# Between two expert layers: every group of tokens coded, POOL scaling all second one-hots, first one-hots of 8 tokens at once on DVE, GELU on 32 tokens

## Chip, cores and metric

One Trainium2 chip, one of its cores. The metric is the device time of one execution in microseconds (us), the median of the runs shown. Engines: PE (TensorE), DVE (VectorE), ACT (ScalarE), POOL (GpSimd) and SP, whose queue here only issues transfers.

## What is computed

256 tokens of width 2048 in f32 go through one block: norm and input projection, pooling and RG-LRU mixers, output projection, and then a retrieval layer over 16,384 experts, the part that matters here:

```python
i1, i2 = top-16 of two score vectors of 128 each      # 8 heads; 128 (i1, i2) pairs per token
expert = i1 * 128 + i2
act    = gelu(einsum('chkd,cd->chk', peer_u[expert], zc))
w      = gate * act
out    = einsum('chk,chkd->cd', w, peer_v[expert])
```

## The kernel before, in words

The kernel doesn't gather most of `peer_u` and `peer_v`. The u layer multiplies z with all 16,384 experts (columns 0 to 1535 as dense matmuls, the rest by gathers) and leaves a table `sw` in SBUF: 128 partitions (first index i1) by 256 tokens by 128 (second index i2). The v layer multiplies such a table, holding the weights, with all of `peer_v`. Between the two, the stage that the diff touches, each token's 128 scores are picked out of its 128x128 square, GELU and gate give 128 weights, and a new square holding the weights at their (i1, i2) is written back to `sw`. Nothing of the v layer's matmuls starts before the last square is written.

The stage works on groups q of 4 tokens, NQ = 64 groups. A loop over steps g does, in an order written out by hand, for group g the picking and for group f = g - LAG the forming:

- `onehot_t(q)`: the first-index one-hot of a group (partition = i1, column = slot) from `ibt`, a copy of the indices broadcast to all partitions by `load_ib` (SP queue). POOL does it by `is_equal` (L874), ACT by Abs and Relu for the groups in `OHT_ACT` (L871, L872). It is issued six groups ahead into five buffers of 8 tokens.
- `extract_mm(q)`: for each token a f32 matmul (two PE instructions) of its one-hot with its square, L940, gives PSUM `exb` [slot, i2]. In two groups of three (`CODED`) a second, bf16 matmul L944 adds an eight-row code (`code_buf`, loaded by `load_code` on SP) times a table, which pushes every column but the wanted one far down.
- `extract_pick(q)`: for a coded group one DVE maximum over the columns for 4 tokens (L952); otherwise for each token a DVE comparison with i2, product and sum (L956).
- `gelu_1`, `gelu_1s`, `gelu_2`, `gelu_2s`, `gelu_3` (L965 to L987): small DVE and ACT instructions for each TB = 16 tokens.
- `one_1(q)`: slot-major one-hot of i1, [128, 4, 128], on ACT for three groups of four (four Abs L998, one Relu L999), else one DVE comparison (L1001). `two_a`, `two_b`: the one-hot of i2 times the weight: for half of the groups DVE compares (L1009) and POOL multiplies (L1016), else four DVE instructions do both (L1020). Both go into `ott`, three buffers each.
- `form_mm(f)`: four f32 matmuls of the two one-hots (L1026), and `form_out(f - 1)`: ACT copies the squares from PSUM to `sw` (L1030).

Each engine runs its instructions in the order issued. `O1_LAST`, `O2_LAST` choose the engines of the last LAG = 8 groups.

Of the kernel before, what the change touches and what calls it, by code (L numbers as in the profile page):

```python
# [16 lines left out]
OP = mybir.AluOpType  # L17
# [25 lines left out]
TB = 16  # L43
LAG = 8
O1_ACT, O2_POOL = (1, 1, 1, 0), (1, 0)
O1_LAST, O2_LAST = (1, 0), (1, 1, 1, 0)
DOT_END = 12
NCODE, FAR = 8, 2.0 ** 120
CODED = (0, 1, 1)
V_MORE, ROOM = 10, 32  # L50
OHT_ACT = (4, 5, 8, 9)
# [103 lines left out]
def kernel(ctx: ExitStack, tc: tile.TileContext, x, cols, front, gates_w, keys, u1, u2, v1, v2,  # L155
# [711 lines left out]
    def onehot_t(q):  # L867

        o, ib = oht(q), ibt[:, q % 4]
        if q in OHT_ACT:  # L870
            nc.scalar.activation(o, ib, AF.Abs, scale=-1.0, bias=pidx)  # L871
            nc.scalar.activation(o, o, AF.Relu, scale=-1.0, bias=1.0)  # L872
        elif q < NQ:
            nc.gpsimd.tensor_scalar(o, ib, pidx, None, op0=OP.is_equal)  # L874
# [3 lines left out]
    for pr in range(64):  # L878
        acc = [bank("mm", 4) for _ in range(2)]
        for kg in range(GU):  # L880
# [15 lines left out]
            if u == nu - DOT_END + 1:  # L896
                assert done[0] == 256
                ibt = zbpool.tile([128, 4, 4, 128], BF, name="ibt", tag="zbhi")
                ohts.append(zbpool.tile([128, 8, 128], F32, name="ohta", tag="zblo"))
                ohts.append(gp.tile([128, 8, 128], F32, name="ohtb", tag="gat"))  # L900
                for q in range(4):
                    load_ib(q)
                for q in range(4):
                    onehot_t(q)
# [10 lines left out]
    pick = asw[:, 3, :].rearrange("p (a b) -> p a b", a=2)  # L915
# [12 lines left out]
    code_buf = [t.rearrange("p a b c -> p (a b c)").bitcast(BF) for t in (i1f, i2f)]  # L928
    coded = [q for q in range(NQ) if CODED[q % len(CODED)]]

    def load_code(n):
        if n < len(coded):
            nc.sync.dma_start(code_buf[n % 2][:NCODE], code_dram[:, coded[n] * 4:coded[n] * 4 + 4, :].rearrange("k t s -> k (t s)"))

    def extract_mm(q):
        p = psE.tile([128, 4, 128], F32, name="exb", bufs=4)
        for j in range(4):
            t = q * 4 + j
            far = q in coded
            nc.tensor.matmul(p[:, j, :].rearrange("p (b i) -> p b i", i=SB), oht(q)[:, j, :], swb[:, :, t, :],  # L940
                             start=True, stop=not far)
            if far:
                n = coded.index(q)
                nc.tensor.matmul(p[:, j, :], code_buf[n % 2][:, j * 128:(j + 1) * 128], ctab, start=False, stop=True)  # L944
        if far:
            load_code(n + 2)
        exb[q] = p

    def extract_pick(q):
        p = exb.pop(q)  # L950
        if q in coded:
            nc.vector.tensor_reduce(act[:, q * 4:q * 4 + 4], p, AX.X, OP.max)  # L952
            return
        for j in range(4):
            t = q * 4 + j
            nc.vector.scalar_tensor_tensor(pick[:, t % 2, :], iota, i2t[:, t:t + 1], p[:, j, :], op0=OP.is_equal,  # L956
                                           op1=OP.mult, accum_out=act[:, t:t + 1])

    gel = {}
    ctab = tv.rearrange("p a b c -> p (a b c)").bitcast(BF)[:, 18 * TB:18 * TB + NK]  # L960
    nc.gpsimd.memset(ctab, 0.0)
    nc.scalar.activation(ctab[:NCODE], wtok[:NCODE, 0, :], AF.Copy)
    gtmp = tv.rearrange("p a b c -> p (a b c)")[:, :9 * TB].rearrange("p (k t) -> p k t", k=9)

    def gelu_1(b):  # L965
        s = slice(b * TB, (b + 1) * TB)
        gel[b] = a, g, c = [gtmp[:, (b % 3) * 3 + j, :] for j in range(3)]
# [3 lines left out]
    def gelu_1s(b):  # L971
        a, g, c = gel[b]
        nc.scalar.activation(g, a, AF.Square)

    def gelu_2(b):
        a, g, c = gel[b]
        nc.vector.tensor_scalar(g, g, GELU_C, 1.0, op0=OP.mult, op1=OP.add)
        nc.vector.tensor_tensor(g, g, a, op=OP.mult)
# [10 lines left out]
    def pick_by(q, most, last):  # L989
        return last[(q - NQ + LAG) % len(last)] if q >= NQ - LAG else most[q % len(most)]  # L990

    def one_1(q):

        o = ott[:, q % 3]
        if pick_by(q, O1_ACT, O1_LAST):
# [3 lines left out]
            nc.scalar.activation(o, o, AF.Relu, scale=-1.0, bias=1.0)  # L999
        else:  # L1000
            nc.vector.tensor_tensor(o, iota[:, None, :].to_broadcast([128, 4, 128]),  # L1001
                                    i1t[:, q * 4:q * 4 + 4].unsqueeze(2).to_broadcast([128, 4, 128]), op=OP.is_equal)

    def o2_pool(q):
        return q >= 6 and pick_by(q, O2_POOL, O2_LAST)

    def two_a(q):
        if o2_pool(q):
            nc.vector.tensor_tensor(ott[:, 3 + q % 3], iota[:, None, :].to_broadcast([128, 4, 128]),  # L1009
                                    i2t[:, q * 4:q * 4 + 4].unsqueeze(2).to_broadcast([128, 4, 128]), op=OP.is_equal)  # L1010

    def two_b(q):

        o = ott[:, 3 + q % 3]
        if o2_pool(q):
            nc.gpsimd.tensor_tensor(o, o, wt[:, q * 4:q * 4 + 4].unsqueeze(2).to_broadcast([128, 4, 128]), op=OP.mult)  # L1016
        else:
            for j in range(4):
                t = q * 4 + j
                nc.vector.tensor_scalar(o[:, j, :], iota, i2t[:, t:t + 1], wt[:, t:t + 1], op0=OP.is_equal,  # L1020
                                        op1=OP.mult)
# [15 lines left out]
    for t in (i1f, i2f):  # L1037
        nc.gpsimd.memset(t, 0.0)
    load_code(0)
    load_code(1)  # L1040
    G = TB // 4
    for g in range(NQ + LAG + 2):
        if g == 0:
            onehot_t(4)
            onehot_t(5)
# [16 lines left out]
        onehot_t(g + 6)  # L1062
        load_ib(g + 8)
        if 0 <= f + 2 < NQ:
            two_a(f + 2)
        if 0 <= f < NQ:
# [218 lines left out]
```

## Time and profile before

| what | value |
|---|---|
| median of 3 runs | 1655.18 us (1652.76 to 1657.89) |
| profiled execution, its time | 1648.98 us |
| its span | 1647.2 us |
| PE, DVE, ACT, POOL busy over the span | 96%, 84%, 54%, 57% |
| the stage between the layers | about 940.8 to 1106.4 us, 165.6 us |

The profiled execution lies 6.2 us below the median. Shares of the whole span say little of this stage, which has one window of its own in the profile: it begins with the first picking matmul (L940) at 940.8 us, the last picking matmul is at 1086.1 us, and the v layer's first ACT instruction (L1117) is at 1106.38 us.

### The profile page before, as it was taken

The page shows a single profiled execution, that of the slowest core. Times are in us where ns is not written, and L with a number is a line of the kernel's source. Part 1 is how long each engine was busy: PE and PEld are TensorE (multiplying, and loading weights), DVE is VectorE, ACT ScalarE, POOL GpSimd, SP SyncE. Part 2 cuts the span into 40 slices and gives each one's busy share as a digit, 9 for nine tenths or more (in the row PEclk, how much of TensorE's full clock was granted, in tenths as well). Part 3 has the DMA queues.
Part 4 walks back from the last instruction along what each step waited for, and adds up shares of the span by engine and source line. Part 5 has one row for each costly group of instructions (what it writes and reads, how often), then busy time and mean ns, then how long its engine had stood idle before and what let it go on. Part 6 is the DMA issues. An engine that isn't in the chain of part 4 may idle for free.

```text
span 1647.2 us, 29352 instructions
## 1 busy us (share of the span) xinstructions
PE 1585.9 (96%) x10646; PEld 1461.2 (89%) x10646; DVE 1378.8 (84%) x2647; ACT 886.1 (54%) x1283; POOL 937.7 (57%) x790
## 2 busy tenths in 40 slices
PE   8899999999999999999999999979999999999996
PEld 8899888989999999999999988878888888888885
DVE  7799755999999997777777499977899998989897
ACT  6665544444444445445444578864545555555554
POOL 2486201346557766555553288846767765666663
PEclk9999999999999999999999999989999999999998
DMA  7455666568988888999998622209999999999992
GB/s 255 150 168 179 204 206 190 180 210 273 313 284 284 276 289 308 325 310 310 306 312 284 199 67 59 57 19 315 313 334 341 350 334 357 360 337 329 351 320 104
DMA packets 129137, 418.43 MB, mean 254 GB/s; under 512 B 18392, under 2 KB 28976, under 8 KB 128864
## 3 DMA queue, kind: packets, MB, share of 16 engines
q1 hardware_dynamic: 86784, 278.52, 51.4%
q0 software_dynamic: 42208, 138.05, 23.7%
q8 instruction: 83, 1.36, 0.3%
q14 instruction: 62, 0.51, 0.1%
HBM read 411.71 MB, written 4.78 MB: 253 GB/s over the span
## 4 chain that ended last, share of the span: by engine, by line
PE 82%; DVE 13%; ACT 2%; issue 1%; POOL 1%; DMA 1%; SPq 0%; ACTq 0%; DVEq 0%; POOLq 0%
PE mm L355 15%; PE mm L354 15%; PE mm L353 15%; PE acc L1144 10%; PE acc L1146 10%; PE acc L1145 10%; DVE ott L1020 3%; DVE lo L109 3%; PE mm L579 2%; PE mm L577 2%; PE mm L578 2%; DVE asw L956 1%; DVE asw L952 1%; DVE ott L1009 1%; ACT hi L108 1%
## 5 line engine op out<-in xcount | busy, mean ns | idle before, releaser
L108 ACT ACTIVATE hi<-raw 128x1024 fp32r<-128x1024 f32 x389 | 411.9, 1059 | 498.4 <-PE mm L354 348.2
L109 DVE TENSOR_TENSOR lo<-raw,hi 128x1024 fp32r<-128x1024 f32 x389 | 504.5, 1297 | 180.2 <-ACT hi L108 178.4
L355 PE MATMUL mm<-zahi,lo 128*128 128x256 f32 x2016 | 574.2, 285 | 15.2 <-DVE lo L109 15.1
L353 PE MATMUL mm<-zahi,hi 128*128 128x256 f32 x2016 | 574.4, 285 | 0.0
L354 PE MATMUL mm<-zalo,hi 128*128 128x256 f32 x2016 | 572.5, 284 | 0.0
L1095 POOL DMA_INDIRECT gatv<-in_v_dram,e x256 | 333.6, 1303 | 178.9 <-DVE accg L1105 114.7
L355 PEld LDWEIGHTS mm<-zahi,lo 128*128 128x128 f32 x2016 | 388.8, 193 | 18.0 <-DVE lo L109 17.8
L353 PEld LDWEIGHTS mm<-zahi,hi 128*128 128x128 f32 x2016 | 389.2, 193 | 0.0
L354 PEld LDWEIGHTS mm<-zalo,hi 128*128 128x128 f32 x2016 | 389.1, 193 | 0.0
L1144 PE MATMUL acc<-hi,wht 128*128 128x512 f32 x512 | 200.3, 391 | 1.8 <-ACT wht L1117 1.8
L1146 PE MATMUL acc<-hi,wlt 128*128 128x512 f32 x512 | 200.3, 391 | 0.0
L1145 PE MATMUL acc<-lo,wht 128*128 128x512 f32 x512 | 200.3, 391 | 0.0
L1105 DVE SCALAR_TENSOR_TENSOR accg<-gatv,wtok,accg 128x512 f32<-128x512 f32 x252 | 183.3, 749 | 2.0 <-DMA gatv<-in_v_dram,e 2.0
L678 POOL DMA_INDIRECT sw<-in_u_dram,e x96 | 112.0, 1167 | 93.0 <-DVE sw L688 46.1
L1144 PEld LDWEIGHTS acc<-hi,wht 128*128 128x128 f32 x512 | 96.6, 189 | 22.2 <-ACT wht L1117 2.1
L1145 PEld LDWEIGHTS acc<-lo,wht 128*128 128x128 f32 x512 | 96.7, 189 | 20.7 <-DVE lo L109 0.6
L1146 PEld LDWEIGHTS acc<-hi,wlt 128*128 128x128 f32 x512 | 96.6, 189 | 20.5 <-DVE wlt L1118 0.6
L1144 PE MATMUL acc<-more,wht 128*128 128x512 f32 x256 | 99.8, 390 | 0.0
L1145 PE MATMUL acc<-more,wht 128*128 128x512 f32 x256 | 99.6, 389 | 0.0
L1146 PE MATMUL acc<-more,wlt 128*128 128x512 f32 x256 | 99.6, 389 | 0.0
L1026 PE MATMUL fob<-ott 128*128 128x128 f32 x512 | 79.1, 296 | 15.7 <-DVE ott L1020 5.4
L678 POOL DMA_INDIRECT gatzbhi<-in_u_dram,e x54 | 61.3, 1136 | 48.2 <-DVE gatzbhi L688 32.6
(288 smaller groups left out, 2729.0 us busy)
## 6 DMA issues: line engine op xcount, KB each, us to landing
raw<-in_u_dram SPq DMA_DIRECT2D x192, 512.0 KB
raw<-in_v_dram SPq DMA_DIRECT2D x125, 512.0 KB
raw<-in_front_dram SPq DMA_DIRECT2D x114, 512.0 KB
sw<-in_v_dram SPq DMA_DIRECT2D x67, 512.0 KB
ibt<-i_dram SPq DMA_DIRECT2D x64, 128.0 KB
gatv<-in_v_dram,e POOLq DMA_INDIRECT x256, 5.9
xh<-in_x_dram SPq DMA_DIRECT2D x8, 256.0 KB
h_dram<-xh POOLq DMA_DIRECT2D x8, 256.0 KB, 3.5
```

What stands on the lines that cost most here:

```text
L108: nc.scalar.activation(s[1], r[1], AF.Copy)
L109: nc.vector.tensor_tensor(s[2], r[1], s[1].bitcast(F32), op=OP.subtract)
L353: nc.tensor.matmul(o, ah, bh, start=first, stop=False)
L354: nc.tensor.matmul(o, ah, bl, start=False, stop=False)
L355: nc.tensor.matmul(o, al, bh, start=False, stop=last)
L678: nc.gpsimd.indirect_dma_start(out=g, out_offset=None, in_=u2, in_offset=bass.IndirectOffsetOnAxis(ap=e32[:, i, sl:sl + 1], axis=0))
L1026: nc.tensor.matmul(p[:, j, :], ott[:, q % 3, j, :], ott[:, 3 + q % 3, j, :], start=True, stop=True)
L1095: nc.gpsimd.indirect_dma_start(out=g, out_offset=None, in_=v2, in_offset=bass.IndirectOffsetOnAxis(ap=e32[:, i, s:s + 1], axis=0))
L1105: nc.vector.scalar_tensor_tensor(a, g, wtok[:, i, s:s + 1], a, op0=OP.mult, op1=OP.add)
L1144: nc.tensor.matmul(acc[i][c], whi[:, j, ts], vh[:, s], start=first, stop=False)
L1145: nc.tensor.matmul(acc[i][c], whi[:, j, ts], vl[:, s], start=False, stop=False)
L1146: nc.tensor.matmul(acc[i][c], wlo[:, j, ts], vh[:, s], start=False, stop=last)
```

## The change

All groups are coded, with four code buffers in place of two, and `extract_pick` is always the one DVE maximum. The second one-hot is for every group a DVE comparison (`two_a`) and a POOL product (`two_b`). The first-index one-hots are made for 8 tokens at once and, but for the first ones (POOL, in the u layer) and the pairs at groups 4 and 8 (ACT), on DVE. The slot-major one-hot of i1 has a third way, "s": POOL subtracts i1 from the column numbers (`one_0`, one step ahead), ACT does Abs and Relu on all 512 columns at once; "a" is the way on ACT alone, "d" the DVE comparison. The groups before the last 12 follow "ssassasd" by q modulo 8 (33 "s", 13 "a", 6 "d"), the last 12 follow "add" by q modulo 3 (4 "a", 8 "d"). GELU takes 32 tokens, in five DVE instructions for six, and LAG grows from 8 to 12.

```diff
--- before.py
+++ after.py
@@ -40,15 +40,14 @@
 GVBUFS = 6
 VIEW_I2 = 64
 SB = 32
-TB = 16
-LAG = 8
-O1_ACT, O2_POOL = (1, 1, 1, 0), (1, 0)
-O1_LAST, O2_LAST = (1, 0), (1, 1, 1, 0)
+TB = 32
+LAG = 12
+O1_BY, O1_LAST = "ssassasd", "add"
+NCB = 4
 DOT_END = 12
 NCODE, FAR = 8, 2.0 ** 120
-CODED = (0, 1, 1)
 V_MORE, ROOM = 10, 32
-OHT_ACT = (4, 5, 8, 9)
+OHT_ACT = (4, 8)
 UNIT_NS, LO_NS, DOT_NS = 2600, 1140, 670
 BUDGET = UNIT_NS - LO_NS
 NG1, GFIRST = 6, 96
@@ -864,14 +863,17 @@
     def oht(q):
         return ohts[q // 2 % NOHT][:, q % 2 * 4:q % 2 * 4 + 4]
 
-    def onehot_t(q):
-
-        o, ib = oht(q), ibt[:, q % 4]
+    def onehot_t(q, eng=None):
+
+        if q >= NQ:
+            return
+        o = ohts[q // 2 % NOHT].rearrange("p a b -> p (a b)")
+        ib = ibt[:, q % 4:q % 4 + 2].rearrange("p a b c -> p (a b c)")
         if q in OHT_ACT:
             nc.scalar.activation(o, ib, AF.Abs, scale=-1.0, bias=pidx)
             nc.scalar.activation(o, o, AF.Relu, scale=-1.0, bias=1.0)
-        elif q < NQ:
-            nc.gpsimd.tensor_scalar(o, ib, pidx, None, op0=OP.is_equal)
+        else:
+            (eng or nc.vector).tensor_scalar(o, ib, pidx, None, op0=OP.is_equal)
 
     nu = 64 * GU
     done0 = done[0]
@@ -900,8 +902,8 @@
                 ohts.append(gp.tile([128, 8, 128], F32, name="ohtb", tag="gat"))
                 for q in range(4):
                     load_ib(q)
-                for q in range(4):
-                    onehot_t(q)
+                for q in (0, 2):
+                    onehot_t(q, nc.gpsimd)
             if u == nu - 3:
                 for q in range(4, 8):
                     load_ib(q)
@@ -912,7 +914,6 @@
 
     asw = cst.tile([128, 4, T], F32, name="asw", tag="zg")
     act, sgt, wt = asw[:, 0, :], asw[:, 1, :], asw[:, 2, :]
-    pick = asw[:, 3, :].rearrange("p (a b) -> p a b", a=2)
     p = bank("tp", 2)
     for i in range(2):
         nc.tensor.transpose(p[:, i * 128:(i + 1) * 128], sg[:, i, :], ident)
@@ -925,57 +926,45 @@
     ott = zpool.tile([128, 6, 4, 128], F32, name="ott", tag="zalo")
 
     exb, fob = {}, {}
-    code_buf = [t.rearrange("p a b c -> p (a b c)").bitcast(BF) for t in (i1f, i2f)]
-    coded = [q for q in range(NQ) if CODED[q % len(CODED)]]
-
-    def load_code(n):
-        if n < len(coded):
-            nc.sync.dma_start(code_buf[n % 2][:NCODE], code_dram[:, coded[n] * 4:coded[n] * 4 + 4, :].rearrange("k t s -> k (t s)"))
+    code_buf = [asw[:, 3, :].bitcast(BF), sg.rearrange("p a b -> p (a b)").bitcast(BF)]
+    code_buf += [t.rearrange("p a b c -> p (a b c)").bitcast(BF) for t in (i1f, i2f)]
+
+    def load_code(q):
+        if q < NQ:
+            nc.sync.dma_start(code_buf[q % NCB][:NCODE],
+                              code_dram[:, q * 4:q * 4 + 4, :].rearrange("k t s -> k (t s)"))
 
     def extract_mm(q):
         p = psE.tile([128, 4, 128], F32, name="exb", bufs=4)
         for j in range(4):
-            t = q * 4 + j
-            far = q in coded
-            nc.tensor.matmul(p[:, j, :].rearrange("p (b i) -> p b i", i=SB), oht(q)[:, j, :], swb[:, :, t, :],
-                             start=True, stop=not far)
-            if far:
-                n = coded.index(q)
-                nc.tensor.matmul(p[:, j, :], code_buf[n % 2][:, j * 128:(j + 1) * 128], ctab, start=False, stop=True)
-        if far:
-            load_code(n + 2)
+            nc.tensor.matmul(p[:, j, :].rearrange("p (b i) -> p b i", i=SB), oht(q)[:, j, :], swb[:, :, q * 4 + j, :],
+                             start=True, stop=False)
+            nc.tensor.matmul(p[:, j, :], code_buf[q % NCB][:, j * 128:(j + 1) * 128], ctab, start=False, stop=True)
+        load_code(q + NCB)
         exb[q] = p
 
     def extract_pick(q):
-        p = exb.pop(q)
-        if q in coded:
-            nc.vector.tensor_reduce(act[:, q * 4:q * 4 + 4], p, AX.X, OP.max)
-            return
-        for j in range(4):
-            t = q * 4 + j
-            nc.vector.scalar_tensor_tensor(pick[:, t % 2, :], iota, i2t[:, t:t + 1], p[:, j, :], op0=OP.is_equal,
-                                           op1=OP.mult, accum_out=act[:, t:t + 1])
+        nc.vector.tensor_reduce(act[:, q * 4:q * 4 + 4], exb.pop(q), AX.X, OP.max)
 
     gel = {}
-    ctab = tv.rearrange("p a b c -> p (a b c)").bitcast(BF)[:, 18 * TB:18 * TB + NK]
+    ctab = tv.rearrange("p a b c -> p (a b c)").bitcast(BF)[:, 12 * TB:12 * TB + NK]
     nc.gpsimd.memset(ctab, 0.0)
     nc.scalar.activation(ctab[:NCODE], wtok[:NCODE, 0, :], AF.Copy)
-    gtmp = tv.rearrange("p a b c -> p (a b c)")[:, :9 * TB].rearrange("p (k t) -> p k t", k=9)
+    gtmp = tv.rearrange("p a b c -> p (a b c)")[:, :6 * TB].rearrange("p (k t) -> p k t", k=6)
 
     def gelu_1(b):
         s = slice(b * TB, (b + 1) * TB)
-        gel[b] = a, g, c = [gtmp[:, (b % 3) * 3 + j, :] for j in range(3)]
+        gel[b] = a, g, c = [gtmp[:, (b % 2) * 3 + j, :] for j in range(3)]
         nc.vector.tensor_tensor(a, act[:, s], sgt[:, s], op=OP.add)
         nc.vector.tensor_tensor(a, a, rstdb[:, s], op=OP.mult)
 
     def gelu_1s(b):
         a, g, c = gel[b]
-        nc.scalar.activation(g, a, AF.Square)
+        nc.scalar.activation(g, a, AF.Square, scale=math.sqrt(GELU_C))
 
     def gelu_2(b):
         a, g, c = gel[b]
-        nc.vector.tensor_scalar(g, g, GELU_C, 1.0, op0=OP.mult, op1=OP.add)
-        nc.vector.tensor_tensor(g, g, a, op=OP.mult)
+        nc.vector.scalar_tensor_tensor(g, g, 1.0, a, op0=OP.add, op1=OP.mult)
         nc.vector.tensor_tensor(c, a, gtt[:, b * TB:(b + 1) * TB], op=OP.mult)
 
     def gelu_2s(b):
@@ -986,39 +975,40 @@
         a, g, c = gel.pop(b)
         nc.vector.scalar_tensor_tensor(wt[:, b * TB:(b + 1) * TB], g, 1.0, c, op0=OP.add, op1=OP.mult)
 
-    def pick_by(q, most, last):
-        return last[(q - NQ + LAG) % len(last)] if q >= NQ - LAG else most[q % len(most)]
+    def rows(i):
+        return iota[:, None, :].to_broadcast([128, 4, 128]), i.unsqueeze(2).to_broadcast([128, 4, 128])
+
+    def o1_by(q):
+        return O1_LAST[q % len(O1_LAST)] if q >= NQ - LAG else O1_BY[q % len(O1_BY)]
+
+    def one_0(q):
+        if o1_by(q) == "s":
+            a, b = rows(i1t[:, q * 4:q * 4 + 4])
+            nc.gpsimd.tensor_tensor(ott[:, q % 3], a, b, op=OP.subtract)
 
     def one_1(q):
 
-        o = ott[:, q % 3]
-        if pick_by(q, O1_ACT, O1_LAST):
+        o, by = ott[:, q % 3], o1_by(q)
+        if by == "d":
+            a, b = rows(i1t[:, q * 4:q * 4 + 4])
+            nc.vector.tensor_tensor(o, a, b, op=OP.is_equal)
+            return
+        if by == "s":
+            nc.scalar.activation(o, o, AF.Abs)
+        else:
             for j in range(4):
                 t = q * 4 + j
                 nc.scalar.activation(o[:, j, :], iota, AF.Abs, scale=-1.0, bias=i1t[:, t:t + 1])
-            nc.scalar.activation(o, o, AF.Relu, scale=-1.0, bias=1.0)
-        else:
-            nc.vector.tensor_tensor(o, iota[:, None, :].to_broadcast([128, 4, 128]),
-                                    i1t[:, q * 4:q * 4 + 4].unsqueeze(2).to_broadcast([128, 4, 128]), op=OP.is_equal)
-
-    def o2_pool(q):
-        return q >= 6 and pick_by(q, O2_POOL, O2_LAST)
+        nc.scalar.activation(o, o, AF.Relu, scale=-1.0, bias=1.0)
 
     def two_a(q):
-        if o2_pool(q):
-            nc.vector.tensor_tensor(ott[:, 3 + q % 3], iota[:, None, :].to_broadcast([128, 4, 128]),
-                                    i2t[:, q * 4:q * 4 + 4].unsqueeze(2).to_broadcast([128, 4, 128]), op=OP.is_equal)
+        a, b = rows(i2t[:, q * 4:q * 4 + 4])
+        nc.vector.tensor_tensor(ott[:, 3 + q % 3], a, b, op=OP.is_equal)
 
     def two_b(q):
 
         o = ott[:, 3 + q % 3]
-        if o2_pool(q):
-            nc.gpsimd.tensor_tensor(o, o, wt[:, q * 4:q * 4 + 4].unsqueeze(2).to_broadcast([128, 4, 128]), op=OP.mult)
-        else:
-            for j in range(4):
-                t = q * 4 + j
-                nc.vector.tensor_scalar(o[:, j, :], iota, i2t[:, t:t + 1], wt[:, t:t + 1], op0=OP.is_equal,
-                                        op1=OP.mult)
+        nc.gpsimd.tensor_tensor(o, o, wt[:, q * 4:q * 4 + 4].unsqueeze(2).to_broadcast([128, 4, 128]), op=OP.mult)
 
     def form_mm(q):
         p = psE.tile([128, 4, 128], F32, name="fob", bufs=3)
@@ -1034,15 +1024,14 @@
         nc.tensor.transpose(p, wt[:, i * 128:(i + 1) * 128], ident)
         nc.scalar.activation(wtok[:, i, :], p, AF.Copy)
 
-    for t in (i1f, i2f):
+    for t in code_buf:
         nc.gpsimd.memset(t, 0.0)
-    load_code(0)
-    load_code(1)
+    for q in range(NCB):
+        load_code(q)
     G = TB // 4
     for g in range(NQ + LAG + 2):
         if g == 0:
             onehot_t(4)
-            onehot_t(5)
 
         def batch(k, *fns):
             if g >= k and (g - k) % G == 0 and (g - k) // G < T // TB:
@@ -1059,10 +1048,13 @@
         if 0 <= f + 1 < NQ:
             one_1(f + 1)
             two_b(f + 1)
-        onehot_t(g + 6)
-        load_ib(g + 8)
+        if g % 2 == 0:
+            onehot_t(g + 6)
+            for q in (g + 10, g + 11) if g else range(8, 12):
+                load_ib(q)
         if 0 <= f + 2 < NQ:
             two_a(f + 2)
+            one_0(f + 2)
         if 0 <= f < NQ:
             form_mm(f)
         if 0 <= f - 1 < NQ:
```

## Rows read from the trace of the kernel before

**Rows 1.** Windows: middle and end of the stage; busy us, counts, granted clock, DMA.
```profile
954.00:1086.20 132.20, 122.57 (x1016) 113.51 (x1015) 130.79 (x424) 106.42 (x289) 108.24 (x76) 1.00 0.20 52
1086.20:1106.40 20.20, 13.44 (x75) 11.98 (x73) 11.54 (x33) 10.88 (x29) 7.73 (x6) 0.75 0.00 0
```

**Rows 2.** Groups by line in the stage, DVE; busy us, mean ns, idle before.
```profile
L1020 DVE TENSOR_SCALAR ott<-iota,i2t,asw 128x128 f32<-128x128 f32 x132 | 48.5, 488 | 0.0
L952 DVE TENSOR_REDUCE asw<-exb 128x4 f32<-128x512 f32 x42 | 28.2, 678 | 1.7 <-PE exb L944 1.7
L956 DVE SCALAR_TENSOR_TENSOR asw<-iota,i2t,exb 128x128 f32<-128x128 f32 x88 | 25.1, 337 | 3.1 <-PE exb L940 3.1
L1009 DVE TENSOR_TENSOR ott<-iota,i2t 128x512 f32<-128x512 f32 x31 | 21.4, 693 | 0.0
```

**Rows 3.** Timeline of PE, a coded and an uncoded group; start us, us.
```profile
945.06 0.22 PE L944 MATMUL exb<-tv,i2f 128*128 128x128 bf16 x1
...
945.39 0.22 PE L944 MATMUL exb<-tv,i2f 128*128 128x128 bf16 x1
945.45 1.11 PE L940 MATMUL exb<-sw,ohtb 128*128 128x128 f32 x8
946.39 0.39 PE L940 MATMUL exb<-sw,oht 128*128 128x128 f32 x2
```

**Rows 4.** Single lines and groups: ns min/median/max, or (L1103, L253) busy us and mean.
```profile
L1020 DVE TENSOR_SCALAR ott<-iota,i2t,asw x132: 332/418/739, 951.8 to 1100.9; 128x128 f32<-128x128 f32 x132
L1103 DVE TENSOR_SCALAR accg<-gatv,wtok 128x512 f32<-128x512 f32 x4 | 1.9, 483 | 0.0
L109 DVE TENSOR_TENSOR lo<-raw,hi x389: 1195/1225/4098, 11.4 to 1627.9; 128x1024 fp32r<-128x1024 f32 x195
L253 POOL TENSOR_TENSOR zg<-xh,g2b 128x512 f32<-128x512 f32 x2 | 2.5, 1288 | 0.0
L978 DVE TENSOR_TENSOR tv<-tv x16: 175/626/1030, 949.9 to 1090.8; 128x16 f32<-128x16 f32 x16
```

**Rows 5.** Groups by line in the stage, ACT.
```profile
L998 ACT ACTIVATE ott<-iota,i1t 128x128 f32<-128x128 f32 x184 | 58.2, 388 | 0.0
...
L999 ACT ACTIVATE ott<-ott 128x512 f32<-128x512 f32 x46 | 29.0, 630 | 1.5
```

**Rows 6.** Groups by line in the stage, POOL.
```profile
L874 POOL TENSOR_SCALAR oht<-ibt,pidx 128x512 f32<-128x512 bf16 x32 | 52.1, 1636 | 18.4 <-PE mm L355 18.4
L1016 POOL TENSOR_TENSOR ott<-ott,asw 128x512 f32<-128x512 f32 x31 | 33.7, 1090 | 29.3 <-DVE ott L1009 26.5 <-DVE tv L977 1.7
```

**Rows 7.** Timeline of DVE and POOL side by side, 976.5 to 979.9 us.
```profile
976.71 1.04 POOL L1016 TENSOR_TENSOR ott<-ott,asw 128x512 f32<-128x512 f32 x1
...
977.73 1.56 POOL L874 TENSOR_SCALAR ohtb<-ibt,pidx 128x512 f32<-128x512 bf16 x1
...
977.82 0.63 DVE L978 TENSOR_TENSOR tv<-tv 128x16 f32<-128x16 f32 x1
...
979.14 0.68 DVE L1001 TENSOR_TENSOR ott<-iota,i1t 128x512 f32<-128x512 f32 x1
979.27 1.97 POOL L874 TENSOR_SCALAR oht<-ibt,pidx 128x512 f32<-128x512 bf16 x1
```

**Rows 8.** Timeline near 1091 us: a small DVE instruction beside a POOL product.
```profile
1090.76 1.04 POOL L1016 TENSOR_TENSOR ott<-ott,asw 128x512 f32<-128x512 f32 x1 [1.65 <-DVE tv L977]
1090.80 1.03 DVE L978 TENSOR_TENSOR tv<-tv 128x16 f32<-128x16 f32 x1
```

**Rows 9.** Timeline near 1095 us: a POOL product beside DVE comparisons.
```profile
1094.67 2.62 POOL L1016 TENSOR_TENSOR ott<-ott,asw 128x512 f32<-128x512 f32 x1 [2.87 <-DVE ott L1009]
...
1095.71 0.69 DVE L1009 TENSOR_TENSOR ott<-iota,i2t 128x512 f32<-128x512 f32 x1
```

**Rows 10.** Group by line in the stage, PE's code matmul of one buffer.
```profile
L944 PE MATMUL exb<-tv,i1f 128*128 128x128 bf16 x84 | 18.4, 219 | 0.9 <-POOL oht L874 0.9
```

**Rows 11.** Windows after the last picking matmul; the granted clock is third from the end.
```profile
1086.20:1094.00 7.80, 5.16 (x39) 4.46 (x38) 7.43 (x25) 5.20 (x16) 3.12 (x3) 1.00 0.00 0
...
1100.00:1106.40 6.40, 5.09 (x23) 4.53 (x21) 1.25 (x5) 3.92 (x10) 0.00 (x0) 0.50 0.00 0
```

## The prediction, on record before the result

> **What bounds the kernel now.** The change touches the stage between the layers and, outside it, only how a few POOL one-hots of the u layer are cut; so the difference must come from the stage's 165.6 us, and I read its windows first: in its middle DVE is busy 130.8 of 132.2 us, PE 122.6, POOL 108.2, ACT 106.4 [rows 1]. DVE is full. The groups by line say with what: 48.5 us go to the second one-hot in four parts (L1020), 25.1 us to the uncoded picks (L956), 28.2 and 21.4 us to the batched maximum and comparison [rows 2]. So the change aims at the engine that bounds. Then I read the timelines of PE, DVE and POOL for what comes next when DVE is relieved: PE, or the access to SBUF for which DVE and POOL seem to wait on each other.
>
> **What PE needs.** Coded, a token takes 0.333 us (945.06 to 945.39), uncoded 0.235 us (four tokens from 945.45 to 946.39) [rows 3]; forming has the same two f32 instructions as an uncoded pick, so 0.235 us. A step is then 4 x (0.333 + 0.235) = 2.27 us, against 1.88 for an uncoded group. Coding the other 22 groups costs PE 22 x 4 x 0.098 = 8.6 us, and 64 groups need 145.4 us of PE: the stage can't fall far below that.
>
> **What DVE is relieved of, and what it gets.** Gone are L1020's 48.5 us, L956's 25.1 and half of the GELU batches. Added are 22 maxima at 0.67 us (28.2/42), 14.7 us; 33 comparisons at 0.68, 22.4 us; and 28 one-hots of 1024 columns. No such one-hot is in the trace. DVE's scalar operation took 0.332 us for 128 columns at its best (L1020) and 0.483 for 512 (L1103), a slope of 0.39 ns a column, which gives 0.68 us for 1024; the two-operand subtraction over 1024 columns took 1.225 us (L109) [rows 4]. I take 0.68, the same kind of operation, with 0.48 (no slope) and 1.23 as the ends. The "d" comparisons (14 for 18) give back 2.7 us. In the middle DVE's own work per step is then 0.67 + 0.68 + 0.34 + 0.09 + 0.1 (GELU) = 1.88 us, under PE's 2.27. ACT: 17 "a" groups at 87.2/46 = 1.9 us and 33 "s" at two passes of 0.63 are 74 us for the 87 us now [rows 5]: no bound either.
>
> **What POOL gets.** It loses its one-hots in the stage (56 of 1.6 us, 32 of them in the row of [rows 6]) and gets 33 more products and 33 subtractions. The subtraction (128x512, one operand constant along the last dimension) is nearest to L1016, whose undisturbed value is 1.04 us [rows 7]; the 128x512 product with two full operands took 1.29 us (L253) [rows 4]. I take 1.04, with 1.29 as the bad end; nothing speaks for less. By busy time alone POOL would have 1.7 us a step, and be free.
>
> **But DVE and POOL exclude each other.** A 16-column DVE product takes 0.175 us at its best [rows 4]. Started 0.04 us after a POOL product, it took 1.03 us and ended 0.03 us after it [rows 8]. It goes the other way too: the POOL product near 1094.67 took 2.62 us and ended 1.58 us after the start of the last of several DVE comparisons [rows 9], that is, 0.54 us of DVE and then its own 1.04. The POOL one-hot that is removed is milder: L978 had got through 0.72 us after its start, of 1.56 us [rows 7].
>
> The Trainium skill (page "SBUF — State Buffer", section "SBUF: two separate sides") says that one port pair is shared by DVE and GpSimd as an exclusive lock, taken by DVE in a two-port mode or with two SBUF inputs, and held for the whole instruction. For the POOL product the trace agrees (1.03 us for 0.175 us of work); for the POOL one-hot it doesn't (0.72 of 1.56 us). The rule speaks against this change, which replaces POOL work that gives way early by POOL work that doesn't; by the rule the time is the sum below, without it that of the first rival.
>
> So I add up the exclusive time in the 52 steps 12 to 63, in which picking and forming overlap. POOL: the products of groups 1 to 52 and 31 subtractions, 83 x 1.02 us (a second POOL instruction starts 1.02 us after a first [rows 7]) = 84.7. DVE: 52 + 7 comparisons. From the start of one, POOL is held 0.54 us (979.14 to 979.27 + 1.97 - 1.56 [rows 7]); one that had to wait has its first 0.12 us behind it when POOL ends, so 0.42 to 0.54 us each, 24.8 to 31.9. One-hots: as a comparison holds 0.14 us less than its 0.68, 23 x 0.54 = 12.4. GELU: six batches of four small two-operand instructions at 0.1, an estimate, 2.4. Sum 124.3 to 131.4 us, 2.39 to 2.53 us a step: just over PE's 2.27. An "s" step needs some 2.8 us and an "a" step 1.8, and the pattern evens out only as far as the three `ott` buffers allow; I take 2.47, above the middle. That makes 52 x 2.47 = 128.4 us.
>
> **Start, end, and what is hidden.** The first 12 steps (8 before) only pick: 12 x 4 x 0.333 = 16.0 us, and I keep the 0.9 us for which PE now waits for a first code [rows 10], as the second code buffer lies in `sg`, which PE reads just before. From 940.8 us to the last pick: 16.9 + 128.4 = 145.3 us. Now it is 145.4: nothing gained. Behind the last pick 12 groups are left to form in place of 8. Now that takes 20.2 us [rows 1], with PE's clock at its half level by 1100 us [rows 11]. Each of the 12 needs 1.02 us of POOL and 1.6 comparisons of 0.42 to 0.54, together 1.75 us, or at the half level twice 0.94 = 1.9 us of PE: 12 x 1.85 = 22.2, and 1.8 for the last eviction and the v layer's first ACT instruction, 24.0.
>
> The 22 added code loads (8 KB each) on SP cost nothing, as each is issued four steps, some 9 us, ahead; were that cover gone, PE would stand at each code matmul, and 64 waits like the one of 0.9 us would be 58 us. The one-hots on DVE stand ahead of `two_a` and the maximum in its queue; behind them come POOL's product and `form_mm`, and that is in the sum. They themselves are six groups ahead of their use. GELU's last step comes one step ahead of the first product that needs it, as now; late by a step, it would stop POOL and PE for some 2 us in each of 8 batches.
>
> Sum: 145.3 + 24.0 = 169.3 for 165.6 us, +3.7 us. On the profiled execution's own 1648.98 us that is 1652.7; on the median, 6.2 us above it, 1659 us.
>
> **Rivals.** (1) *PE sets the pace*: POOL's instructions hold SBUF for less than their record. For it: PE's 2.27 is only 0.12 below the lower end of the sum. Against it: [rows 8, 9]. The middle would be 118.0 us, the end 21 (PE less often late): 16.9 + 118.0 + 21 = 156, -10 us, 1645 us. It decides once a POOL instruction costs 0.95 us of exclusive time in place of 1.02 (78.9 + 24.8 + 12.4 + 2.4 = 118.5). (2) *The waits add up*: DVE stands behind two POOL instructions in a row, its maximum comes late too, and "a" steps can't make up for "s" steps. Then five steps of 2.9 and three of 2.29 in eight make 2.67 a step, and the end keeps the 2.3 us a group that it has now, 28 us: 16.9 + 138.8 + 28 = 184, +18 us, 1673 us. The one-hot at its bad price alone gives 23 x 0.55 = +13. For it: POOL waits for DVE 26.5 us now [rows 6]. Against it: three buffers, and no chain that closes within one step. (3) *PE's clock falls in the middle*: at half of it a step is 4.54 us, so ten such steps cost 21 us. Against it: the middle leaves PE 92% busy, and at 5.16 of 7.8 us it still had its full level [rows 11].
>
> **How the numbers follow.** The sum's case (-3 to +10 us, 1652 to 1665) has a chance of 0.46, rival 1 (-14 to -4) 0.27, rival 2 (+10 to +25) 0.22, rival 3 0.05. About 0.3%, 5 us, is what a measurement of this kernel can tell from no change. Of the sum's case 0.03 is faster, 0.26 the same and 0.17 slower; of rival 1, 0.23 is faster and 0.04 the same; the other two are slower: 0.26, 0.30 and 0.44. The predicted time is the sum's, 1659 us. The range takes in most of rival 1 and the lower half of rival 2, which also holds the bad ends of the one-hot and of the subtraction (33 x 0.25 = 8 us): 1644 to 1678 us; the sum's own is 1652 to 1665.
>
> **What would show it.** In the profile after: DVE's comparisons and one-hots well above 0.68 us and its small products up to 1 us, POOL's instructions above 1.04 us, by their waits on each other; steps of 2.4 to 2.5 us up to a last pick near 1086 us; then 24 us more, at the half clock at the end. Steps of 2.27 us with PE without gaps would be rival 1. The prediction fails if the one-hot takes 1 us or more undisturbed, if the end takes 30 us, or if the subtraction isn't priced like the product.

## The result, and the profile after

The changed kernel took 1661.29 us (median of 10 runs, 1656.7 to 1668.32) against 1654.15 us for the kernel before (10 runs, 1648.36 to 1657.89): a ratio of 1.0052, 95% interval 1.0033 to 1.0071, so 5 to 12 us slower. 1659 us was forecast. The profiled execution took 1660.88 us, with a span of 1659.1 us.

The span is 11.9 us longer than before, but not all of that is the change. The stage begins 6.5 us later (947.3 us for 940.8), behind the same matmuls; over the 13 profiles of this study its start lies anywhere from 940.8 to 947.3 us, and what follows the stage takes 538.3 to 541.4 us. I therefore compare the stage itself: from the first picking matmul (L940) to the v layer's first ACT instruction it takes 172.0 us for 165.6, 6.4 us more. From the first to the last picking matmul it is 148.1 us (145.3 before, to the start of the last such matmul in both), the end 23.9 (20.3).

The windows of the changed kernel, from the first forming matmul to the last pick and then in two pieces to the end (busy us of PE, PE's weight loads, DVE, ACT, POOL; granted clock, DMA share, GB/s), answer to [rows 1, 11]:

```profile
966.70:1095.40 128.70, 119.00 (x1022) 110.96 (x1022) 127.60 (x165) 88.68 (x192) 104.53 (x84) 1.00 0.18 49
...
1095.40:1104.00 8.60, 6.05 (x40) 5.70 (x38) 7.81 (x14) 5.16 (x15) 5.79 (x5) 0.83 0.00 1
1104.00:1119.20 15.20, 10.06 (x70) 8.32 (x68) 12.26 (x11) 10.23 (x25) 10.24 (x8) 0.99 0.01 2
```

DVE is as full as before, 127.6 of 128.7 us, though the work taken from it was more than the work given to it. The groups by line in the stage show with what it is full (busy us, mean ns of one, idle before; for [rows 2, 6]):

```profile
L1011 POOL TENSOR_TENSOR ott<-ott,asw 128x512 f32<-128x512 f32 x64 | 79.3, 1245 | 46.2 <-DVE ott L1006 44.4 <-PE fob L1016 1.9
...
L1006 DVE TENSOR_TENSOR ott<-iota,i2t 128x512 f32<-128x512 f32 x64 | 67.3, 1055 | 0.2 <-PE fob L1016 0.2
...
L987 POOL TENSOR_TENSOR ott<-iota,i1t 128x512 f32<-128x512 f32 x33 | 45.8, 1389 | 0.0
...
L947 DVE TENSOR_REDUCE asw<-exb 128x4 f32<-128x512 f32 x64 | 43.3, 679 | 4.5 <-PE exb L942 4.5
...
L876 DVE TENSOR_SCALAR oht<-ibt,pidx 128x1024 f32<-128x1024 bf16 x16 | 17.4, 1087 | 2.3 <-DMA ibt<-i_dram 2.3
```

The maximum, which reads PSUM, has the 0.68 us that it had. The comparison, which reads two operands in SBUF, has a mean of 1.06 us where it had 0.69, and POOL's product 1.25 where it had 1.09. The same lines one by one (ns minimum, median, maximum) tell that no instruction became longer by itself; each still has its short value:

```profile
L1006 DVE TENSOR_TENSOR ott<-iota,i2t x64: 676/1032/1526, 964.8 to 1114.7; 128x512 f32<-128x512 f32 x64
L1011 POOL TENSOR_TENSOR ott<-ott,asw x64: 1033/1041/1626, 965.6 to 1116.3; 128x512 f32<-128x512 f32 x64
L987 POOL TENSOR_TENSOR ott<-iota,i1t x33: 1032/1486/1590, 948.0 to 1092.2; 128x512 f32<-128x512 f32 x33
L876 DVE TENSOR_SCALAR oht<-ibt,pidx x16: 741/924/1577, 947.7 to 1069.3; 128x1024 f32<-128x1024 bf16 x16
```

In the timeline of DVE and POOL the two pass SBUF to and fro (start us, us; for [rows 7 to 9]):

```profile
1010.73 1.04 POOL L1011 TENSOR_TENSOR ott<-ott,asw 128x512 f32<-128x512 f32 x1 [0.63 <-DVE ott L1006]
1011.17 1.15 DVE L1006 TENSOR_TENSOR ott<-iota,i2t 128x512 f32<-128x512 f32 x1
1011.73 1.49 POOL L987 TENSOR_TENSOR ott<-iota,i1t 128x512 f32<-128x512 f32 x1
1012.24 0.68 DVE L947 TENSOR_REDUCE asw<-exb 128x4 f32<-128x512 f32 x1
```

The comparison of 1011.17 is stopped by the product until 1011.77 and ends 0.55 us later, at 1012.32; the subtraction is stopped until the comparison has read, some 0.45 us; the maximum runs beside it undisturbed.

### The profile page after: what moved, and what is told of

It reads as the page before. It is cut to its first block, busy times and chain, and to the rows that moved or that the text cites. A ratio compares the mean times of both kernels' runs of the same rounds, so it can differ in the third digit from the quotient of the medians.

```text
span 1659.1 us, 29221 instructions
## 1 busy us (share of the span) xinstructions
PE 1592.8 (96%) x10734; PEld 1467.3 (88%) x10734; DVE 1384.4 (83%) x2362; ACT 869.7 (52%) x1184; POOL 929.4 (56%) x800
## 4 chain that ended last, share of the span: by engine, by line
PE 80%; DVE 8%; POOL 3%; DMA 3%; issue 3%; ACT 2%; SPq 0%; another core or an unknown queue 0%; DVEq 0%; ACTq 0%; POOLq 0%
PE mm L354 14%; PE mm L353 14%; PE mm L352 13%; PE acc L1138 10%; PE acc L1137 10%; PE acc L1136 10%; DVE lo L108 3%; PE mm L578 2%; PE mm L576 2%; PE mm L577 2%; POOL ott L1011 2%; DVE ott L1006 1%; DMA raw<-in_u_dram 1%; ACT hi L107 1%; PE fob L1016 1%
## 5 line engine op out<-in xcount | busy, mean ns | idle before, releaser
L354 PE MATMUL mm<-zahi,lo 128*128 128x256 f32 x2016 | 575.5, 285 | 17.3 <-DVE lo L108 17.2
L1087 POOL DMA_INDIRECT gatv<-in_v_dram,e x256 | 320.9, 1254 | 185.5 <-DVE accg L1097 131.7
L1138 PEld LDWEIGHTS acc<-hi,wlt 128*128 128x128 f32 x512 | 96.5, 188 | 20.8 <-DVE wlt L1110 0.8
L1011 POOL TENSOR_TENSOR ott<-ott,asw 128x512 f32<-128x512 f32 x64 | 79.3, 1245 | 46.2 <-DVE ott L1006 44.4
L1016 PE MATMUL fob<-ott 128*128 128x128 f32 x512 | 74.1, 290 | 16.8 <-POOL ott L1011 13.6
```

The source lines that it names most:

```text
L354: nc.tensor.matmul(o, al, bh, start=False, stop=last)
L1087: nc.gpsimd.indirect_dma_start(out=g, out_offset=None, in_=v2, in_offset=bass.IndirectOffsetOnAxis(ap=e32[:, i, s:s + 1], axis=0))
L1138: nc.tensor.matmul(acc[i][c], wlo[:, j, ts], vh[:, s], start=False, stop=last)
```

## The experiments

Theory A is the prediction's: DVE's instructions with two operands in SBUF, its one-hots and POOL's instructions exclude each other, and their sum, 2.47 us a step, paces the stage where PE would need 2.27. Theory B, the rival, takes the profile at its face: DVE is full, so DVE's own work paces the stage. A third reading, that PE's load paces it, is weighed where it differs. The table gives for each kernel, in us of the profiled execution, the start (from the first picking to the first forming matmul), the middle (from there to the last picking matmul), the two together ("to last pick"), the end behind it and the stage; then the ratio to the kernel before with its interval. A difference of two ratios is uncertain by some 0.3%.

| kernel | start | middle | to last pick | end | stage | ratio (95%) |
|---|---|---|---|---|---|---|
| before | 11.8 | 133.5 | 145.3 | 20.3 | 165.6 | 1 |
| changed | 19.4 | 128.7 | 148.1 | 23.9 | 172.0 | 1.0052 (1.0033 to 1.0071) |
| no_sub | 22.3 | 113.5 | 135.8 | 23.3 | 159.1 | 0.9946 (0.9927 to 0.9965) |
| all_sub | 22.3 | 136.9 | 159.2 | 23.9 | 183.1 | 1.0086 (1.0066 to 1.0106) |
| iota_psum | 20.8 | 113.4 | 134.2 | 18.0 | 152.2 | 0.9923 (0.9903 to 0.9943) |
| lag8 | 16.5 | 146.3 | 162.8 | 17.0 | 179.8 | 1.0079 (1.0059 to 1.0100) |
| tb16 | 20.2 | 136.0 | 156.2 | 24.7 | 180.9 | 1.0092 (1.0066 to 1.0118) |
| half_scale | 21.0 | 120.9 | 141.9 | 23.8 | 165.7 | 1.0017 (1.0005 to 1.0029) |
| before_psum | 13.6 | 129.6 | 143.2 | 16.2 | 159.4 | 0.9964 (0.9949 to 0.9979) |
| psum_uncode | 18.2 | 114.0 | 132.2 | 18.5 | 150.7 | 0.9905 (0.9880 to 0.9931) |
| uncode | 18.0 | 131.2 | 149.2 | 24.4 | 173.6 | 1.0054 (1.0037 to 1.0070) |
| oh_pool | 25.1 | 162.6 | 187.7 | 23.9 | 211.6 | 1.0268 (1.0233 to 1.0303) |
| psum_sixth | 18.0 | 112.9 | 130.9 | 17.9 | 148.8 | 0.9891 (0.9862 to 0.9921) |

The start differs between profiles in which PE has the same work to do there. Five microseconds of it, from 3 us into the stage on, in the changed kernel and in no_sub:

```profile
950.30:955.30 5.00, 5.00 (x47) 4.83 (x47) 2.77 (x4) 0.81 (x1) 0.00 (x0) 1.00 0.43 109
...
948.40:953.40 5.00, 5.00 (x26) 4.50 (x25) 1.39 (x2) 0.00 (x0) 0.00 (x0) 0.50 0.28 87
```

In no_sub PE's clock was at its half level, and PE got through 26 matmuls in place of 47. The same stretch, 3 to 8 us into the stage, has 0.50 in all_sub and 0.66 to 0.75 in iota_psum, lag8, half_scale, before_psum and oh_pool. What decides it isn't shown; it is worth up to 3 us (22.3 for 19.4). So differences of a few microseconds to the last pick are read from the middle, which has 51 steps (55 with a lag of 8).

**no_sub and all_sub: less and more of POOL's work.**

```diff
-O1_BY, O1_LAST = "ssassasd", "add"
+O1_BY, O1_LAST = "aaad", "add"       # no_sub
+O1_BY, O1_LAST = "s", "add"          # all_sub
```

> The changed kernel without POOL's subtractions: before the last 12 groups the pattern is 'aaad' in place of 'ssassasd'. Theory A (DVE's comparisons and one-hots and POOL's instructions exclude each other, and their sum paces the middle): the exclusive sum falls from 2.47 to about 1.9 us a step, below PE's 2.27, so the middle goes from 128.7 to 118 us, comparisons on DVE come near 0.7 us, and the kernel is 10 us faster than the changed one. Theory B (DVE's instructions are that long by themselves and DVE, busy 127.6 of 128.7 us, paces the middle by its own work): 6 or 7 more comparisons at 1.05 us make the middle some 6 us longer.

> The changed kernel with POOL's subtraction for every group before the last 12 (52 in place of 33). Theory A: the exclusive sum becomes 102 POOL instructions x 1.02 plus 53 comparisons, 2.75 to 2.85 us a step, so the middle is 143 to 148 us and the kernel 14 to 19 us slower than the changed one. Theory B: six comparisons fewer on DVE, POOL alone would need only 2.04 us a step: about 6 us faster.

Without the subtractions the time to the last pick falls by 12.3 us, although DVE got seven comparisons more; with 19 more it rises by 11.1, although DVE lost six. Both go against theory B in sign. The middle alone is 15.2 us shorter and 8.2 us longer. In all_sub that is about half of what theory A's sum gives, 19 x 1.02 us less 6 x 0.42 to 0.54, that is, 16 to 17 us (14 to 19 were expected). Why it is less isn't shown. Idle exclusive time that the added work filled would explain it, but the timeline of the changed kernel's middle shows little: POOL's instructions and DVE's comparisons, one-hots and GELU cover 126.8 of the 128.7 us, their waits for each other included. The windows of the two middles show PE at its limit in no_sub, and DVE as full as ever, which is a warning not to read that column by itself; in all_sub POOL is nearly full too:

```profile
967.70:1081.20 113.50, 113.50 (x1023) 111.09 (x1021) 113.08 (x171) 94.30 (x250) 54.05 (x52) 1.00 0.22 55
...
964.20:1101.10 136.90, 122.18 (x1023) 110.89 (x1021) 134.35 (x159) 89.50 (x164) 133.77 (x102) 1.00 0.17 46
```

**iota_psum: the comparisons' exclusion taken away, the work left.** The column numbers that DVE compares with are copied once to a free part of a PSUM bank. Every instruction stays; POOL goes on reading them from SBUF.

```diff
+    aux = psE.tile([128, 512], F32, name="aux", bufs=1)
+    iop = aux[:, 256:384]
+    nc.vector.tensor_copy(iop, iota)
...
-    def rows(i):
-        return iota[:, None, :].to_broadcast([128, 4, 128]), i.unsqueeze(2).to_broadcast([128, 4, 128])
+    def rows(i, io=None):
+        return (iop if io is None else io)[:, None, :].to_broadcast([128, 4, 128]), i.unsqueeze(2).to_broadcast([128, 4, 128])
...
-        p = psE.tile([128, 128], F32, name="wtp", bufs=1)
+        p = aux[:, :128]
```

> The changed kernel, but the column numbers that DVE's comparisons read lie in PSUM (a free part of the bank that the weight transposes use), so each comparison has one operand in SBUF in place of two. Theory A: comparisons fall from a mean of 1.05 us to about 0.7, POOL's from 1.25 and 1.39 to near 1.04; only the one-hots and GELU's small instructions still exclude POOL; PE paces the middle at 2.27 us a step, 118 us, and the end gets shorter by about 4 us: 10 to 15 us faster than the changed kernel. Theory B: no change beyond 2 us.

The stage is 19.8 us shorter than in the changed kernel, the end 5.9 us of it. By the ratios the gain is 1.3%, 21 us, more than the 10 to 15 expected. Groups by line:

```profile
L1014 POOL TENSOR_TENSOR ott<-ott,asw 128x512 f32<-128x512 f32 x64 | 69.9, 1101 | 43.2 <-DVE ott L1009 43.0
...
L1009 DVE TENSOR_TENSOR ott<-aux,i2t 128x512 f32<-128x512 f32 x64 | 43.4, 680 | 2.2 <-PE fob L1019 1.5 <-ACT wtok L1028 0.3 <-issue 0.3
L990 POOL TENSOR_TENSOR ott<-iota,i1t 128x512 f32<-128x512 f32 x33 | 35.6, 1078 | 1.9 <-PE fob L1019 1.8
```

The comparison's mean is now 0.68 us, its best value in the changed kernel, so reading PSUM neither shortened nor lengthened the instruction itself, and 24 us of DVE's time are gone from that one line (67.3 to 43.4). The timeline has the direct proof, a comparison begun 0.44 us into a product and not delayed by it, and the small GELU instruction L970, which still has two operands in SBUF, waiting for another product:

```profile
1010.37 1.04 POOL L1014 TENSOR_TENSOR ott<-ott,asw 128x512 f32<-128x512 f32 x1 [1.23 <-DVE ott L1009]
1010.81 0.65 DVE L970 SCALAR_TENSOR_TENSOR tv<-tv 128x32 f32<-128x32 f32 x1
...
1015.51 1.04 POOL L1014 TENSOR_TENSOR ott<-ott,asw 128x512 f32<-128x512 f32 x1 [1.23 <-DVE ott L1009]
1015.95 0.68 DVE L1009 TENSOR_TENSOR ott<-aux,i2t 128x512 f32<-128x512 f32 x1
```

The middle is now PE's, without a gap, at full clock, with every POOL instruction and the longer way of the "s" one-hots (POOL, then ACT) still there, so it wasn't these by themselves that paced the changed kernel. The end keeps the full clock too; that isn't what shortened it, as tb16 and oh_pool have ends of 24.7 and 23.9 us at a clock of 1.00:

```profile
964.60:1078.00 113.40, 113.40 (x1023) 111.03 (x1021) 104.71 (x164) 89.42 (x193) 89.91 (x84) 1.00 0.20 55
1078.00:1096.00 18.00, 14.43 (x108) 12.62 (x107) 12.11 (x23) 14.64 (x36) 11.27 (x11) 1.00 0.01 2
```

64 picks and 52 formings at [rows 3]'s prices are 85.2 + 48.9 = 134.1 us; measured are 134.2. That agreement is luck: only 51 formings stand before the last pick, the start took 20.8 us where its 13 picks are priced at 17.3, and a step of the gapless middle takes 113.4 / 51 = 2.22 us, not 2.27.

**lag8 and tb16: the lag and GELU's batches.**

```diff
-TB = 32
-LAG = 12
+TB = 16       # lag8 and tb16
+LAG = 8       # lag8
```

> The changed kernel with GELU on 16 tokens and the lag of 8 groups as before (TB = 16, LAG = 8). The exclusive sum per step is the same but for GELU's second batch. Theory A: 56 steps at 2.47 us in the middle, 8 picking steps ahead and 8 groups behind: 14 + 138.6 + 16 = 169 us for the stage in place of 172.0, 2 to 4 us faster than the changed kernel. Rival: the longer lag is what lets POOL trail PE, and without it the middle gets longer, so the kernel is slower than the changed one.

> The changed kernel with GELU on 16 tokens, the lag of 12 kept; it splits the two parts of the run with TB = 16 and LAG = 8, whose time from the first to the last pick grew by 14.7 us. If GELU's batches are the cause (each of a batch's small DVE instructions with two SBUF operands waits for a POOL instruction, and DVE stands meanwhile), the time from the first to the last pick is 8 to 14 us above the 148.1 us of the changed kernel. If the shorter lag is the cause (POOL can no longer trail PE), it stays within 2 us of 148.1.

My expectation of lag8 missed: a gain of 3 us was expected, and the stage became 7.8 us longer. tb16 splits it. With the lag of 12 kept, the time to the last pick is 8.1 us above the changed kernel's, 7.3 of it in the middle. A step of the middle takes 136.0 / 51 = 2.67 us in tb16 and 146.3 / 55 = 2.66 in lag8, against 2.52 in the changed kernel: GELU's batches make the step longer, and the lag doesn't matter for it. The shorter lag only moves four groups from the end into the middle, and lag8's end gives them back (17.0 us). Eight batches more are 40 small DVE instructions more. The profile of tb16 has many of them at several times their best, the one below, for example, at a median of 964 ns where the same instruction took 175 in the kernel before (the last line):

```profile
L959 DVE TENSOR_TENSOR tv<-tv,rstdb 128x16 f32<-128x16 f32 x16 | 13.1, 816 | 0.5
...
L959 DVE TENSOR_TENSOR tv<-tv,rstdb x16: 174/964/966, 953.6 to 1104.7; 128x16 f32<-128x16 f32 x16
...
L969 DVE TENSOR_TENSOR tv<-tv,rstdb x16: 174/175/177, 948.0 to 1089.3; 128x16 f32<-128x16 f32 x16
```

So one of the change's parts, GELU on 32 tokens, is worth some 7 to 8 us in it.

**half_scale and oh_pool: two parts of the change undone.** half_scale gives back to DVE, ahead of the last 12 groups, every other second one-hot (four instructions, compare and multiply); oh_pool leaves the one-hots of 8 tokens on POOL.

```diff
+    def o2_pool(q):                                     # half_scale; else as in the kernel before
+        return q >= NQ - LAG or (q >= 6 and q % 2 == 0)
...
-            (eng or nc.vector).tensor_scalar(o, ib, pidx, None, op0=OP.is_equal)
+            nc.gpsimd.tensor_scalar(o, ib, pidx, None, op0=OP.is_equal)      # oh_pool
```

> The changed kernel, but the second one-hot is made as in the kernel before for every other group ahead of the last 12 (four DVE instructions, compare and multiply), so that POOL scales 26 groups fewer. Theory A: 26 POOL instructions fewer (26.5 us of exclusive time) against 26 x 0.5 us more on DVE, 0.26 us a step less; PE then paces the middle, and from the first to the last pick it takes 136 to 140 us in place of 148.1: 8 to 12 us faster than the changed kernel. Rival: DVE, whose own work becomes 2.1 us a step and which still waits for POOL, stays full, and the time stays within 3 us.

> The changed kernel with the first-index one-hots of 8 tokens left on POOL, as before the change; this undoes one part. POOL then has 23 one-hots of about 2.9 us more in the middle, 3.1 us of its own work a step, more than PE's 2.27 and the 2.47 of the changed kernel: POOL paces it, and from the first to the last pick it takes 175 to 190 us in place of 148.1, so the kernel is 27 to 42 us slower than the changed one. If DVE's own work were what counts (theory B), it would be 10 to 20 us faster, as DVE loses 31 us of one-hots.

Undoing a part of POOL's scaling makes the changed kernel 0.35% faster and the stage 6.3 us shorter, the difference to the kernel before. So this part costs what the whole change lost, but it isn't the only one: no_sub, which takes the subtractions from POOL, gives back 12.9 us of the stage. The 6.2 us to the last pick are less than the 8 to 12 expected; the middle alone has 7.8. The one-hots of oh_pool are the opposite: left on POOL they make it 2.1% slower than the changed kernel (1.0268 for 1.0052), 36 us, against theory B, which had it faster; and the windows have POOL busy 163.67 of 165 us. With POOL scaling all the second one-hots, moving these to DVE was needed.

```profile
965.00:1130.00 165.00, 130.65 (x1017) 121.53 (x1017) 90.27 (x140) 89.77 (x193) 163.67 (x109) 0.92 0.15 39
```

**before_psum: the same edit to the kernel before.** The edit of iota_psum, in the three lines L1001, L1009 and L1020.

> The kernel before, with only the column numbers of DVE's comparisons (both kinds of second one-hot, and the first) read from PSUM. If waits on POOL were a part of what kept DVE full before the change too, L1020 falls from 0.418 to about 0.33 us and the stage from 165.6 to 152 to 157 us, near the 152.2 us of the changed kernel with the same edit: then the change's own parts bring next to nothing once the exclusion is gone. If DVE was full by its own work, the stage stays within 4 us of 165.6.

The stage becomes 159.4 us, 6.2 less, between the two cases. In the main line, L1020 of before, the mean falls from 488 to 400 ns only:

```profile
L1023 DVE TENSOR_SCALAR ott<-aux,i2t,asw 128x128 f32<-128x128 f32 x132 | 44.8, 400 | 0.0
...
L1023 DVE TENSOR_SCALAR ott<-aux,i2t,asw x132: 392/401/409, 956.5 to 1100.6; 128x128 f32<-128x128 f32 x132
```

Minimum, median and maximum tell why: it no longer waits at all (409 ns at most, 739 before [rows 4]), but its best value rose from 332 to 392 ns. In the timeline four of them in a row take 1.35 to 1.37 us here; before they took 1.10 at best and mostly 1.57 to 1.68. Waits on POOL were thus a part of what kept DVE full before too, in this line some 12 of its 48.5 us (33 x 1.10 = 36.3, an estimate), and the edit put some 8 us (33 x 0.25) of longer instructions in their place. With the same edit the changed kernel needs 152.2 us, 7.2 less. As the changed kernel has no such four-part instruction, that isn't the price of the change's parts alone.

**uncode, psum_uncode, psum_sixth: the code matmuls.** One group in three (six in the last) is picked without code again, as L956 did.

```diff
-NCB = 4
+NCB = 3
+CODED = (0, 1, 1)                     # psum_sixth: (0, 1, 1, 1, 1, 1)
...
-        nc.vector.tensor_reduce(act[:, q * 4:q * 4 + 4], exb.pop(q), AX.X, OP.max)
+        p = exb.pop(q)
+        if q in coded:
+            nc.vector.tensor_reduce(act[:, q * 4:q * 4 + 4], p, AX.X, OP.max)
+            return
+        for j in range(4):
+            t = q * 4 + j
+            nc.vector.scalar_tensor_tensor(pick[:, t % 2, :], iota, i2t[:, t:t + 1], p[:, j, :], op0=OP.is_equal,
+                                           op1=OP.mult, accum_out=act[:, t:t + 1])
```

> The changed kernel with one group in three picked without code, as before the change; this undoes another part. It takes 8.6 us from PE and gives DVE 0.13 us a step more that doesn't exclude POOL. Theory A with DVE in order: DVE is full with its waits (127.6 of 128.7 us), so the 8.8 us more on it show almost whole: from the first to the last pick 150 to 157 us in place of 148.1, and the kernel is 2 to 9 us slower than the changed one. If PE's load were what counts, it would be up to 8 us faster.

> The changed kernel with the comparisons' column numbers in PSUM, and one group in three picked without code as before the change. There PE paced the time from the first to the last pick (134.2 us). If the code matmuls cost PE 22 x 4 x 0.098 us as the prediction has it, that time falls by 8 us to 126, and the kernel is 7 to 8 us faster than the one with only the PSUM edit, as DVE's 8.8 us more still fit under PE. If DVE comes full by it, the gain is under 3 us.

> The changed kernel with the comparisons' column numbers in PSUM and one group in six picked without code. With all coded PE paced it (134.2 us from the first to the last pick), with one in three uncoded DVE was full (132.2 us). One in six takes 4.3 us from PE and gives DVE 4.4 us, for which DVE has room: 130 to 131 us, 1 to 2 us less than either, and the fastest kernel of the study at about 0.990 of the kernel before.

In the changed kernel it makes little difference (uncode: +1.1 us to the last pick, the same ratio), below the 2 to 9 us expected and against the reading that PE's load paces it. In the middle 17 groups are uncoded, 17 x 0.4 = 6.8 us (8.8 / 22 = 0.4) more of DVE's own work, and it is 2.5 us longer. The uncoded pick, with its scores in PSUM, never waits for POOL:

```profile
L960 DVE SCALAR_TENSOR_TENSOR asw<-iota,i2t,exb x88: 333/336/347, 944.8 to 1095.3; 128x128 f32<-128x128 f32 x88
```

With the column numbers in PSUM, psum_uncode missed the 7 to 8 us expected. It is 2 us shorter to the last pick, but not in the middle (114.0 for 113.4 us), where DVE is full:

```profile
960.60:1074.60 114.00, 110.41 (x952) 105.27 (x953) 112.65 (x284) 88.38 (x192) 88.51 (x84) 1.00 0.21 54
```

The 2 us come from the start, where five of 13 groups have no code and the clock stayed at its full level. One in six (psum_sixth) has the 130.9 us to the last pick that were expected, but by the start too: 2.8 of its 3.3 us on iota_psum lie there, and the middle is 112.9 for 113.4. Its median, 1632.54 us against 1649.96 of the kernel before beside it, is the lowest ratio of the study, 0.9891, but the intervals of iota_psum and psum_uncode overlap it: that uncoding any groups helps isn't shown.

## Why the prediction was right, point by point

- *The step of PE*, 2.27 us: near, 2% too long; the gapless middles of iota_psum and no_sub take 2.22 us a step. The price of the code matmuls shows in no total time: uncode and psum_uncode have DVE full.
- *The exclusive sum*, 2.47 us a step: from the first forming matmul, less its own pick of 1.33 us, to the last pick it was 130.0 us for 52 steps, 2.50. The exclusion is shown as the cause by no_sub, all_sub and iota_psum. The sum as a price is not: the work added in all_sub moved the middle by 8.2 us where the sum gives 16 to 17. 2.47 lay near the measured step partly by luck, as I had chosen it above the sum's middle by judgement.
- *The one-hot on DVE*: taken at 0.68, at its best 0.74. *The subtraction* like the product: at its best 1.03. Near and right.
- *The start*: 12 picking steps took 18.1 us (966.7 - 1.3 - 947.3) for the 16.9 forecast. The wait that I had kept at 0.9 us is 1.6 us ahead of the first code matmul, on the load of the first code buffer, and not behind `sg`; the rest lies in smaller waits.
- *The end*: 24.0 us forecast, 23.9 measured, in part by luck: the 1.85 us a group were set between 1.75 by the exclusion and 1.9 by PE at its half clock. PE's clock did not stay at its half level (0.83 in the first 8.6 us, then 0.99); a forming then takes 1.16 us, and the end is still as long because comparisons and products take turns there. Without the exclusion it took 18.0 us.
- *GELU at 0.1 us an instruction*, 2.4 us in all, was too little as a price on DVE: each small instruction may stand for a whole product. tb16 puts eight batches at 7 to 8 us.
- *The sum*: +3.7 us forecast, +6.4 us in the stage and 5 to 12 us in the runs. The 2.7 us missing are 1.2 in the start and 1.6 in the middle.
- *Rival 1* (PE sets the pace) is what iota_psum and no_sub turn the kernel into; *rival 2* (waits adding up to 2.67) and *rival 3* (the clock) did not happen; the middle's clock was 1.00.

What the change was to bring went there: DVE was relieved of its own work, and the new POOL work made it wait for as much and more. With the column numbers in PSUM in both kernels the changed one is 7.2 us ahead in the stage; with them in SBUF it is 6.4 us behind.

## What to carry to other kernels

Before work is moved from DVE to POOL, add up the time in which both need two accesses to SBUF, as if it were one engine's; here it came to 2.5 us a step with neither engine's own work above 1.9. It told the pace of the change to come, within 2%, but put the further work of all_sub at twice what it cost. If that sum is above the bound, try one operand of the DVE instruction in PSUM before moving anything: a few lines gave 21 us here. Look at the instruction's best time after it, too: the 128x512 comparison kept its 0.68 us, the 128-column compare and multiply rose from 0.33 to 0.39. And a full DVE in the profile says nothing by itself: compare each line's median with its minimum.

## What was not expected of the hardware

- A DVE comparison with one operand in PSUM ran beside a POOL product without any delay (0.68 us, begun 0.44 us into 1.04), so for this instruction it is the second SBUF operand, not the engine, that excludes.
- The one-hot on DVE excludes though it has only one tensor operand, in SBUF, and a column of scalars. In iota_psum, begun 0.64 us into a subtraction, it took 0.95 us for a best of 0.74, and the product behind took 1.49 for 1.04:

```profile
1016.50 1.04 POOL L990 TENSOR_TENSOR ott<-iota,i1t 128x512 f32<-128x512 f32 x1
1017.14 0.95 DVE L876 TENSOR_SCALAR ohtb<-ibt,pidx 128x1024 f32<-128x1024 bf16 x1
1017.50 1.49 POOL L1014 TENSOR_TENSOR ott<-ott,asw 128x512 f32<-128x512 f32 x1
```

- The 4-part instruction of the kernel before (compare and multiply, 128 columns) stopped waiting when its data operand moved to PSUM, though its two scalar operands stayed in SBUF, and its own time rose from 332 to 392 ns.
- PE's clock kept 0.99 in the last 15 us of the stage with PE busy 10.1 of 15.2 us, where it had been at 0.50 in the last 6 us before the change [rows 11] with PE busy 5.1 of 6.4; the fall there came in a stretch with PE busy 3.19 of 6 us, at 0.70:

```profile
1094.00:1100.00 6.00, 3.19 (x17) 2.99 (x16) 2.87 (x5) 1.76 (x5) 4.62 (x3) 0.70 0.00 0
```
